# Start addresses of TensorE's operands moved to multiples of 512 bytes, and two small reorderings in the convolution layer of a four-layer decoder

## The chip, the cores and the metric

The kernel runs on one core of one Trainium2 chip. The metric is device time in microseconds (us) of one execution, the median of several runs. A profiled execution of the same program gives the trace; times in it are us from the start of its span, and single instructions are given in ns.

## The reference

Four layers work on x, 256 tokens by 1024 features, fp32. Each layer adds a token mixer and then an MLP with a squared ReLU:

```python
for i in range(DEPTH):                       # DEPTH = 4
    h = _rms_norm(x, attn_norm[i])
    y = mixer[i](h, ...)                     # 0: sparse attention, 1: stick-breaking attention,
                                             # 2: Conformer convolution, 3: block-sparse attention
    x = x + y
    hm = _rms_norm(x, mlp_norm[i])
    x = x + jnp.square(jax.nn.relu(hm @ mlp_w_up[i])) @ mlp_w_down[i]   # 1024 -> 4096 -> 1024
```

The mixer of layer 2, in which code is moved:

```python
a, b = jnp.split(h @ w_in, 2, axis=-1)
u = a * jax.nn.sigmoid(b)                    # gate
u = causal_depthwise_conv(u, dw_w, width=31) + dw_b
un = (u - mean(u)) * rsqrt(var(u) + eps) * ln_g + ln_b
return jax.nn.silu(un) @ w_out
```

## The kernel before

Weights come from HBM in transfers of 1 MB (tile `raw`, 128 partitions by 2048 fp32). ScalarE (ACT) rounds them to fp32r (`wh`, line 157), VectorE (DVE) takes the remainder (`wl`, line 158). Activations are held in the same way as a high and a low part (`xT`, `oT`, `u`). A product of two such numbers is three matmuls: high by high, low by high, high by low. TensorE loads a stationary operand of 128 columns (row kind PEld in the profile) and streams a moving operand of up to 512 columns past it (row kind PE); each matmul here loads its own stationary operand.

The matmuls that matter by name:

- `projT` (line 211, `proj_T`): first half of each MLP and some mixer projections. Stationary: slices of `wh` or `wl`; moving: `xT`, 512 columns with `wh` (high and low part of x in one go) and 256 with `wl`.
- `dn` (lines 190 to 192, `mm3`): second half of each MLP. Stationary: `u`; moving: 512 columns of `wh` or `wl`.
- `proj` (the same lines): mixer projections. Stationary: `xT`; moving: mostly 512 columns of `wh` or `wl`.
- `acc` (lines 218 to 220, `mm3_T`): mixer outputs. `ab` (line 917): the convolution's input product. Both: stationary `wh`/`wl`, moving 256 columns.
- fp32 matmuls (transposes against `ident`, products with `mean`, attention scores) move a column at half the rate, and all of them but the transposes show as two records each.

Tiles are laid out in SBUF one after the other, in the order in which pools and tiles are made: the pool `const` (`xr`, `gains`, `ident`, `nhalf`, `mean`, `identr`), then `rawp`, `hlp` (`wh`, `wl`), `act` (`xT`, `oT`, sums of squares), `sm` (small ones), and above them the pools that one stage opens and closes. So a small tile early on shifts all that follow. All tiles start at multiples of 32 bytes. Read from the built program, in bytes past a multiple of 512:

| tile | before | after |
|---|---|---|
| `wh`, `wl`, `raw` | 416 | 0 |
| `xT`, `oT` | 416 | 0 |
| `u` in the MLPs of layers 0, 2 and 3 | 32 | 0 |
| `u` in the MLP of layer 1 | 96 | 0 |
| `mean`, `identr` | 416 | 0 |
| `ident` | 384 | 0 |
| `qT`, `kT`, `vv`, exponentials of layer 1 | 32 | 0 |
| `un`, `uc` of the convolution | 448 | 352 |

Slices of `wh`, `wl`, `xT` and `u` begin at further multiples of 512 bytes, so they have the tile's remainder. One exception is the fourth chunk of layer 0's projection, 280 columns wide (1120 bytes): there the moving slices for an odd feature tile start at 416 + 1120 = 3 x 512 bytes, and those for an even one at 416.

Each engine executes its own list in order. The lists are made by a scheduling layer from the order of the code and `issue_after`; it may put independent work between.

In `conv`, the norm of the input is needed as a row factor `rbc` before the first gate. `token_stats` makes two tiny products `ms` (sums of squares by `mean`), GpSimd (POOL) raises them to the power -1/2 (`rstd`, line 128), `broadcast_rows` makes `bc` by TensorE. The gate's VectorE, ScalarE and DMA work leads to `us`. After that come `fill` (matmuls whose result nobody reads, line 947), then five steps of 1, 1, 2, 2 and 2 feature tiles: normalise `un` on VectorE (line 953), transpose it on TensorE (line 960), silu on ScalarE (line 963, twice a tile: rounded and exact), the low part on VectorE (line 966). The output product `o.go` reads `oT`; the weights of its second half are split only after the last silu.

Of the kernel before, what the change touches and what calls it, by code (L numbers as in the profile page):

```python
# [10 lines left out]
F32 = mybir.dt.float32  # L11
F32R = mybir.dt.float32r
# [4 lines left out]
P = 128  # L17
# [3 lines left out]
KT = D // P  # L21
# [46 lines left out]
def trunk(ctx: ExitStack, tc: tile.TileContext, A: dict, out: bass.AP):  # L68
    nc = tc.nc
    const = ctx.enter_context(tc.tile_pool(name="const", bufs=1))  # L70
    rawp = ctx.enter_context(tc.tile_pool(name="rawp", bufs=3))
    hlp = ctx.enter_context(tc.tile_pool(name="hlp", bufs=8))
    act = ctx.enter_context(tc.tile_pool(name="act", bufs=2))
    sm = ctx.enter_context(tc.tile_pool(name="sm", bufs=4))
    ps = ctx.enter_context(tc.tile_pool(name="ps", bufs=2, space=bass.MemoryType.PSUM))

    def bank(tag, name):
        return ps.tile([P, 512], F32, tag=tag, bufs=4 if tag == "B" else 2, name=name)


    def start_norm(i):
        n = Norm()
        n.g = gains[:, i]
        n.xT = act.tile([P, KT, 2, NT, P], F32R, tag="aT", name="xT")
        n.s2 = act.tile([P, S], F32, tag="s2", name="s2")
        return n
# [24 lines left out]
    def token_stats(n, tag):  # L111

        o = bank(tag, "ms")
        for t in range(NT):
            nc.tensor.matmul(o[:, 2 * t:2 * t + 2], lhsT=n.s2[:, t * P:(t + 1) * P], rhs=mean[:, 0:2], start=t == 0,
                             stop=t == NT - 1, skip_group_check=True)
        n.me = sm.tile([P, NT], F32, tag="nme", name="nme")
        nc.vector.tensor_scalar(n.me, o[:, 0:2 * NT].rearrange("p (t c) -> p t c", c=2)[:, :, 0], EPS, None,
                                op0=ALU.add)
# [6 lines left out]
    def rstd(n):  # L126
        r = sm.tile([P, NT], F32, tag="rstd", name="rstd")
        nc.gpsimd.tensor_tensor(r, n.me, nhalf[:, :NT], op=ALU.pow)
        return [r[:, t:t + 1] for t in range(NT)]

    def broadcast_rows(dst, cols, tag):

        o = bank(tag, "bc")
        for t in range(NT):
            nc.tensor.matmul(o[:, t * P:(t + 1) * P], lhsT=cols[t].to_broadcast([P, P]), rhs=ident, start=t == 0,
                             stop=t == NT - 1, skip_group_check=True)
        if dst is None:
            return o
        nc.scalar.copy(dst, o[:, :S])
# [75 lines left out]
    def mm3_T(o, w, aT, kt, first, last):  # L215

        wh, wl = w
        nc.tensor.matmul(o, lhsT=wh, rhs=aT[:, kt, 0], start=first, stop=False, skip_group_check=True)  # L218
        nc.tensor.matmul(o, lhsT=wh, rhs=aT[:, kt, 1], start=False, stop=False, skip_group_check=True)  # L219
        nc.tensor.matmul(o, lhsT=wl, rhs=aT[:, kt, 0], start=False, stop=last, skip_group_check=True)  # L220

    class Acc:
# [3 lines left out]
            self.b = {}  # L226

        def add(self, m, w, aT, kt, first, last):
            if m // 2 not in self.b:
                self.b[m // 2] = bank("AC"[m // 4], f"acc{m // 2}")  # L230
            fs = slice(m * P, (m + 1) * P)
            mm3_T(self.tile(m), (w[0][:, fs], w[1][:, fs]), aT, kt, first and m % 2 == 0, last)

        def tile(self, m):
            return self.b[m // 2][:, (m % 2) * S:(m % 2 + 1) * S]

    class Out:
# [13 lines left out]
        def fetch(self, i, eng):  # L251

            self.raws[i] = rawp.tile([P, 2048], F32, tag="raw", name="raw")
            eng.dma_start(self.raws[i], self.src[:, i * 2048:(i + 1) * 2048])

        def go(self, kts, ms):
            last = KT - 1 in kts
# [562 lines left out]
    def conv(n):  # L820
        aT = n.xT
        nxt = start_norm(6)
        with tc.tile_pool(name="cv", bufs=1) as sp, tc.tile_pool(name="cvw", bufs=2) as wp, \
# [11 lines left out]
            rbc = sp.tile([P, S], F32, name="rbc")  # L835
# [69 lines left out]
            for c in range(4):  # L905

                v = ahead.pop(0)
                if c < 3:
                    ahead.append(col_chunk(A["conv_w"], (c + 1) * 4096, 512))
                os_ = [bank("B", "ab") for f in range(2)]  # L910

                def products(f, kts):
                    for i in range(2):
                        fs = slice((2 * i + f) * P, (2 * i + f + 1) * P)
                        for kt in kts:
                            for m, (wi, xi) in enumerate(((0, 0), (0, 1), (1, 0))):
                                nc.tensor.matmul(os_[f][:, i * S:(i + 1) * S], lhsT=v[kt][wi][:, fs],  # L917
                                                 rhs=aT[:, kt, xi], start=kt == 0 and m == 0 and i == 0,
                                                 stop=kt == KT - 1 and m == 2, skip_group_check=True)

                if c == 0:

                    for kts in (range(4), range(4, 8)):
                        for f in range(2):
                            products(f, kts)
                    first = os_
                    continue
                for f in range(2):
                    products(f, range(KT))
                    if c == 1 and f == 0:  # L930
                        token_stats(n, "C")
                        broadcast_rows(rbc, rstd(n), "C")
                        gate(0, first[0])
                        gate(1, first[1])
                    gate(2 * c + f, os_[f])
# [7 lines left out]
            o = outs[0]  # L943

            fill = bank("C", "fill")
            for _ in range(FILL):
                nc.tensor.matmul(fill[:, :P], lhsT=mean, rhs=mean, start=True, stop=True)
            for c0, w in STEPS:
                h = slice(c0, c0 + w)
                un = wp.tile([P, 2, NT, P], F32, tag="ab", name="un")  # L950
                pt = bank("B", "un")
                for e in range(NT):
                    nc.vector.tensor_scalar(un[:, :w, e].rearrange("p k (g q) -> p k g q", q=16),
                                            us[:, h].rearrange("p k (g e q) -> p k e g q", e=2, q=16)[:, :, e],
                                            mv[:, e, 0:1], rs[:, e:e + 1], op0=ALU.subtract, op1=ALU.mult)
                ac = wp.tile([P, 2, S], F32, tag="ac", name="ac")
                for k in range(w):
                    for e in range(NT):
                        x = (NT * k + e) * P
                        nc.tensor.transpose(pt[:, x:x + P], un[:, k, e], ident)  # L960

                    for dst in (oT[:, c0 + k, 0].rearrange("p t c -> p (t c)"), ac[:, k]):
                        a = nc.scalar.activation(dst.rearrange("p (j e) -> p e j", e=2),
                                                 pt[:, k * S:(k + 1) * S].rearrange("p (e j) -> p e j", e=2), AF.Silu,
                                                 scale=cw[:, c0 + k, 2:3], bias=cw[:, c0 + k, 3:4])
                b = nc.vector.tensor_sub(oT[:, h, 1], ac[:, :w].rearrange("p k (t c) -> p k t c", c=P),
                                         oT[:, h, 0].bitcast(F32))
                if c0 + w == LATE:
                    with tc.issue_after(a.ins), tc.issue_after(b.ins):
                        o.load(range(EARLY, 4))  # L970
            raw = rawp.tile([P, 2048], F32, tag="raw", name="raw")
            with tc.issue_after(power.ins):
                nc.gpsimd.dma_start(raw, A["up2"][:, :2048])
            o.go(range(4), range(8))
            o.go(range(4, 8), range(8))
        return nxt, raw

# [1 line left out]
    def moba(n):  # L979
# [114 lines left out]
                o.go(range(4, 8), range(8))  # L1094
        return nxt

    xr = const.tile([P, KT, S], F32, name="xr")
    gains = const.tile([P, 8, KT], F32, name="gains")
    ident = const.tile([P, P], F32, name="ident")
    nc.scalar.dma_start(gains, A["norms"])  # L1100
    nc.scalar.dma_start(ident, A["ident"])
    nhalf = const.tile([P, 4], F32, name="nhalf")
    nc.vector.memset(nhalf, -0.5)
    mean = const.tile([P, P], F32, name="mean")
    nc.vector.memset(mean, 1.0 / D)
    n = start_norm(0)
    feats = list(range(KT))
# [10 lines left out]
    o = bank("C", "warm")  # L1118
    for _ in range(10):
        nc.tensor.matmul(o[:, :P], lhsT=mean, rhs=mean, start=True, stop=True)  # L1120

    identr = const.tile([P, P], F32R, name="identr")
    n = nsa(n, load_x)
    n = mlp(0, n, 1)
    n = stick(n)
    taps = {}
    with tc.tile_pool(name="taps", bufs=1) as tapp:
        tp = tapp.tile([P, KT, 64], F32, name="tp")
        nc.sync.dma_start(tp, A["conv_taps"])
        eye = tapp.tile([P, 16], F32, name="eye")  # L1130
        nc.sync.dma_start(eye, A["eye16"])
        n = mlp(1, n, 2, lambda j: taps_tile(j) if j < 4 else None)
        n, raw = conv(n)
    n = mlp(2, n, 3, None, raw)
    n = moba(n)
# [121 lines left out]
```

## Time and profile before

| | |
|---|---|
| median of 3 runs | 1180.42 us (1180.06 to 1180.87) |
| the profiled execution | 1180.44 us |
| its span, first to last instruction of the program | 1178.7 us |
| TensorE busy | 1167.1 us, 7046 records |
| VectorE, ScalarE busy | 782.9 us, 620.9 us |
| HBM read | 207.74 MB |

A matmul's record lasts from its start to the modelled end of its result, and the next one starts while it lasts; records overlap. The busy share of TensorE therefore says that it is hardly ever empty, not how fast it streams. What one matmul costs the ones behind it is the time from its start to the next start, called its step below. It is read from the start times of a first and a last row and the count between them.

### The profile page before, as it was taken

How to read it: one execution, taken by the hardware profiler on the slowest of the kernel's cores; microseconds unless marked ns; L12 is line 12 of the kernel's file. 1: busy time of each engine (PE TensorE's matmuls, PEld its weight loads, DVE VectorE, ACT ScalarE, POOL GpSimd, SP SyncE). 2: the span in 40 equal slices, each digit the busy share in tenths (PEclk: the TensorE clock that was granted, in tenths of full speed). 3: DMA queues.
4: the chain of work that ended last, by engine and by line, in shares of the span. 5: the costliest groups of instructions: out<-in, count | busy, mean ns of one | idle time of the engine just before them, and what ended most of it. 6: DMA issues, size and time to landing. Idle time of an engine off the chain costs nothing.

```text
span 1178.7 us, 17661 instructions
## 1 busy us (share of the span) xinstructions
PE 1167.1 (99%) x7046; PEld 1008.7 (86%) x7046; DVE 782.9 (66%) x1206; ACT 620.9 (53%) x1031; POOL 33.2 (3%) x50
## 2 busy tenths in 40 slices
PE   9999999999999999999999999999999999999998
PEld 6798988888888998888889998888888889888886
DVE  7788675656585686656665677656659886656553
ACT  6487554444565654544563275454446665544441
POOL 1100000000000000000001100000001100000000
PEclk9999999999999999999999999999999999999999
DMA  8554255545454436545545746455455543555440
GB/s 303 203 186 144 77 210 214 185 172 204 154 201 163 144 129 222 190 183 198 188 151 165 251 172 222 164 197 212 153 195 178 182 162 118 187 214 192 165 178 36
DMA packets 35650, 211.11 MB, mean 179 GB/s; under 512 B 4592, under 2 KB 7664, under 8 KB 12016
## 3 DMA queue, kind: packets, MB, share of 16 engines
q1 hardware_dynamic: 31104, 198.76, 47.0%
q0 software_dynamic: 1568, 6.80, 2.1%
q10 hardware_dynamic: 2896, 4.42, 1.1%
q8 instruction: 55, 0.90, 0.3%
q14 instruction: 27, 0.22, 0.1%
HBM read 207.74 MB, written 2.23 MB: 178 GB/s over the span
## 4 chain that ended last, share of the span: by engine, by line
PE 67%; issue 26%; DVE 3%; ACT 2%; DMA 1%; POOL 1%; SPq 0%; POOLq 0%; ACTq 0%; DVEq 0%
PE projT L211 23%; PE dn L190 8%; PE dn L192 8%; PE dn L191 8%; PE ab L917 2%; PE proj L192 2%; PE proj L191 2%; PE proj L190 2%; PE acc L218 2%; PE acc L220 2%; PE acc L219 2%; DVE wl L158 1%; PE po L675 1%; ACT wh L157 1%; PE cv L859 1%
## 5 line engine op out<-in xcount | busy, mean ns | idle before, releaser
L158 DVE TENSOR_TENSOR wl<-raw,wh 128x1024 fp32r<-128x1024 f32 (+1 forms) x372 | 441.1, 1212 | 186.9 <-ACT wh L157 182.8
L157 ACT CAST wh<-raw 128x1024 fp32r<-128x1024 f32 (+1 forms) x372 | 376.1, 1041 | 215.6 <-PE dn L192 111.2
L211 PE MATMUL projT<-xT,wh 128*128 128x512 f32 x1152 | 361.5, 396 | 0.3 <-DVE xT L101 0.3
L211 PEld LDWEIGHTS projT<-xT,wl 128*128 128x128 f32 x1152 | 215.3, 188 | 49.9
L211 PE MATMUL projT<-xT,wl 128*128 128x256 f32 x1152 | 225.4, 278 | 0.0
L190 PE MATMUL dn<-wh,u 128*128 128x512 f32 x512 | 202.7, 396 | 0.0
L192 PE MATMUL dn<-wh,u 128*128 128x512 f32 x512 | 202.0, 395 | 0.0
L191 PE MATMUL dn<-wl,u 128*128 128x512 f32 x512 | 201.4, 393 | 0.0
L211 PEld LDWEIGHTS projT<-xT,wh 128*128 128x128 f32 x1152 | 178.2, 189 | 3.7 <-DVE xT L101 0.5
L192 PEld LDWEIGHTS dn<-wh,u 128*128 128x128 f32 x512 | 96.4, 188 | 22.4
L191 PEld LDWEIGHTS dn<-wl,u 128*128 128x128 f32 x512 | 96.4, 188 | 20.7
L190 PEld LDWEIGHTS dn<-wh,u 128*128 128x128 f32 x512 | 96.5, 188 | 20.4
L316 ACT COPY b<-projT 128x256 f32<-128x256 f32 x128 | 41.2, 374 | 93.7 <-PE projT L211 93.4
L191 PE MATMUL proj<-wl,xT 128*128 128x512 f32 (+2 forms) x224 | 85.9, 384 | 2.5 <-DVE wl L158 2.1
L190 PE MATMUL proj<-wh,xT 128*128 128x512 f32 (+2 forms) x224 | 85.7, 385 | 0.4 <-ACT wh L165 0.3
L317 DVE TENSOR_TENSOR s<-projT,b 128x256 f32<-128x256 f32 x128 | 48.2, 418 | 55.0 <-ACT b L316 55.0
L192 PE MATMUL proj<-wh,xT 128*128 128x512 f32 (+2 forms) x224 | 84.5, 378 | 0.0
L89 ACT CAST u<-q 128x1024 fp32r<-128x1024 f32 x32 | 33.6, 1049 | 82.9 <-DVE q L319 82.7
L218 PE MATMUL acc<-oT,wh 128*128 128x256 f32 x256 | 73.8, 292 | 0.0
L219 PE MATMUL acc<-oT,wh 128*128 128x256 f32 x256 | 72.7, 285 | 0.0
L220 PE MATMUL acc<-oT,wl 128*128 128x256 f32 x256 | 71.2, 284 | 0.0
L90 DVE TENSOR_TENSOR u<-q,u 128x1024 fp32r<-128x1024 f32 x32 | 39.2, 1226 | 34.5 <-ACT u L89 34.5
(231 smaller groups left out, 1252.6 us busy)
## 6 DMA issues: line engine op xcount, KB each, us to landing
raw<-in_down SPq DMA_DIRECT2D x64, 1024.0 KB, 4.8
raw<-in_up SPq DMA_DIRECT2D x63, 1024.0 KB, 4.8
raw<-in_sb_w SPq DMA_DIRECT2D x12, 1024.0 KB, 4.8
raw<-in_moba_w SPq DMA_DIRECT2D x12, 1024.0 KB, 4.9
raw<-in_conv_w SPq DMA_DIRECT2D x8, 1024.0 KB, 4.7
st<-dr POOLq DMA_DIRECT2D x16, 287.0 KB, 6.3
raw<-in_nsa_w SPq DMA_DIRECT2D x4, 1024.0 KB, 5.9
rawc<-in_nsa_cmp SPq DMA_DIRECT2D x4, 1024.0 KB, 4.8
```

The costliest lines, as they stand in the source:

```text
L90: return a, nc.vector.tensor_sub(lo, src, hi.bitcast(F32))
L157: nc.scalar.copy(wh[:, :w], r)
L158: nc.vector.tensor_sub(wl[:, :w], r, wh[:, :w].bitcast(F32))
L190: nc.tensor.matmul(o, lhsT=aT[:, kt, 0, t, :], rhs=wh, start=first, stop=False)
L191: nc.tensor.matmul(o, lhsT=aT[:, kt, 0, t, :], rhs=wl, start=False, stop=False)
L192: nc.tensor.matmul(o, lhsT=aT[:, kt, 1, t, :], rhs=wh, start=False, stop=last)
L211: nc.tensor.matmul(o[:, :width], lhsT=v[kt][part][:, f * P:(f + 1) * P], rhs=rhs, start=kt == 0 and part == 0, stop=kt == KT - 1 and part ...
L218: nc.tensor.matmul(o, lhsT=wh, rhs=aT[:, kt, 0], start=first, stop=False, skip_group_check=True)
L219: nc.tensor.matmul(o, lhsT=wh, rhs=aT[:, kt, 1], start=False, stop=False, skip_group_check=True)
L220: nc.tensor.matmul(o, lhsT=wl, rhs=aT[:, kt, 0], start=False, stop=last, skip_group_check=True)
L316: nc.scalar.copy(b, o[:, S:])
L317: nc.vector.tensor_add(s[:, f], o[:, :S], b)
```

## The change

Tiles are reordered, widened or added so that the operands of the large matmuls start at multiples of 512 bytes (table above). An unused tile `front` of 384 bytes stands ahead of `const`, one named `back` of 384 bytes follows `sm`; `ident`, `identr` and `mean` stand next to each other, `nhalf` is widened to 256 bytes and `eye` to 512. Of the program's 6523 matmuls none had both operands at a multiple of 512 before, and 5866 have after.

In `conv`, `token_stats` and `rstd` move ahead of the products of the second chunk. `Out.begin` issues the 24 output matmuls of the first feature tile in the middle of the five steps, and the transposes of the third step may only be issued behind the first 16 of them.

```diff
+    edge = ctx.enter_context(tc.tile_pool(name="edge", bufs=1))
+    edge.tile([P, 96], F32, name="back")
...
+        def begin(self, parts):
+            for wi, xi in parts:
+                for m in range(KT):
+                    p = nc.tensor.matmul(self.acc.tile(m), lhsT=self.w[0][wi][:, m * P:(m + 1) * P],
+                                         rhs=self.aT[:, 0, xi], start=wi + xi == 0 and m % 2 == 0, stop=False,
+                                         skip_group_check=True)
+            return p
...
+                if c == 1:
+                    token_stats(n, "C")
+                    rows = rstd(n)
                 for f in range(2):
                     products(f, range(KT))
                     if c == 1 and f == 0:
-                        token_stats(n, "C")
-                        broadcast_rows(rbc, rstd(n), "C")
+                        broadcast_rows(rbc, rows, "C")
...
-                        nc.tensor.transpose(pt[:, x:x + P], un[:, k, e], ident)
+                        with ExitStack() as behind:
+                            if c0 == 2:
+                                behind.enter_context(tc.issue_after(begun[0].ins))
+                            nc.tensor.transpose(pt[:, x:x + P], un[:, k, e], ident)
...
+                if c0 < 2:
+                    begun.append(o.begin(((0, 0), (1, 0)) if c0 == 0 else ((0, 1),)))
...
-            o.go(range(4), range(8))
+            o.go(range(1, 4), range(8))
...
+    const.tile([P, 96], F32, name="front")
     xr = const.tile([P, KT, S], F32, name="xr")
+    ident = const.tile([P, P], F32, name="ident")
+    identr = const.tile([P, P], F32R, name="identr")
+    mean = const.tile([P, P], F32, name="mean")
     gains = const.tile([P, 8, KT], F32, name="gains")
-    nhalf = const.tile([P, 4], F32, name="nhalf")
+    nhalf = const.tile([P, 64], F32, name="nhalf")
...
-        eye = tapp.tile([P, 16], F32, name="eye")
+        eye = tapp.tile([P, P], F32, name="eye")[:, :16]
```

On TensorE's list of the program before, at the end of the first half of the second chunk of `conv`, the sums `ms` and the broadcast `bc` stand close together among the products `ab`:

```order
L917 MATMUL ab<-xT,wl 128x256
L115 MATMUL ms<-mean,s_4340 128x2 x2
L917 MATMUL ab<-xT,wh 128x256 x2
L917 MATMUL ab<-xT,wl 128x256
L917 MATMUL ab<-xT,wh 128x256
L135 MATMUL bc<-ident,rstd 128x128 x2
L917 MATMUL ab<-xT,wh 128x256
```

Of the changed program, TensorE's list near the start of that chunk's products (three rows) and near the end of their first half (three rows):

```order
L928 MATMUL ab<-xT,wl 128x256
L117 MATMUL ms<-mean,s_4345 128x2 x2
L928 MATMUL ab<-xT,wh 128x256 x2
...
L928 MATMUL ab<-xT,wl 128x256
L137 MATMUL bc<-ident,rstd 128x128 x2
L928 MATMUL ab<-xT,wh 128x256 x2
```

The two `ms` products moved up by 42 products `ab`, and `bc` by 4.

On TensorE's list of the program before, at the convolution's output behind `fill` (`un` is the transposes of the five steps, `acc` the output's matmuls, the number that of an accumulator):

```order
L947 MATMUL fill<-mean 128x128 x11
L960 MATMUL un<-ident,un 128x128 x8
L218 MATMUL acc_6847<-oT,wh 128x256
L218 MATMUL acc_6854<-oT,wh 128x256
L218 MATMUL acc_6861<-oT,wh 128x256
L218 MATMUL acc_6868<-oT,wh 128x256
```

The same place of the changed program:

```order
L960 MATMUL fill<-mean 128x128 x11
L977 MATMUL un<-ident,un 128x128 x4
L262 MATMUL acc_6782<-oT,wh 128x256 x2
L262 MATMUL acc_6785<-oT,wh 128x256 x2
...
L262 MATMUL acc_6791<-oT,wh 128x256 x2
L977 MATMUL un<-ident,un 128x128 x4
L220 MATMUL acc_6782<-oT,wh 128x256
```

The third step's four transposes stood with the first four; now 24 output matmuls (12 rows of 2, of which nine are left out) stand between.

## Rows read from the trace of the kernel before

**Rows 1.** The page's head and busy times (us, share of span, records).

```profile
span 1178.7 us, 17661 instructions
PE 1167.1 (99%) x7046; PEld 1008.7 (86%) x7046; DVE 782.9 (66%) x1206; ACT 620.9 (53%) x1031; POOL 33.2 (3%) x50
```

**Rows 2.** Busy time in one MLP block of layer 2, with granted clock.

```profile
750.38:772.68 22.30, 22.30 (x114) 18.77 (x113) 13.41 (x15) 10.34 (x14) 0.00 (x0) 1.00 0.52 189
```

**Rows 3.** Groups by line and shape: count, busy us, mean ns of a record, idle.

```profile
L211 PE MATMUL projT<-xT,wh 128*128 128x512 f32 x1152 | 361.5, 396 | 0.3 <-DVE xT L101 0.3
L211 PE MATMUL projT<-xT,wl 128*128 128x256 f32 x1152 | 225.4, 278 | 0.0
L190 PE MATMUL dn<-wh,u 128*128 128x512 f32 x512 | 202.7, 396 | 0.0
L218 PE MATMUL acc<-oT,wh 128*128 128x256 f32 x256 | 73.8, 292 | 0.0
...
L190 PE MATMUL proj<-wh,xT 128*128 128x512 f32 x176 | 69.6, 398 | 0.4 <-ACT wh L165 0.3
```

**Rows 4.** Timeline of TensorE, MLP of layer 2: start, length, line, operands.

```profile
741.79 0.39 PE L211 MATMUL projT<-xT,wl 128*128 128x256 f32 x2
...
750.38 0.39 PE L190 MATMUL dn<-wh,u 128*128 128x512 f32 x1
...
761.54 0.39 PE L211 MATMUL projT<-xT,wh 128*128 128x512 f32 x1
```

**Rows 5.** Timeline of TensorE, MLP of layer 1: first `dn`, and the row behind the 48th.

```profile
497.66 0.40 PE L190 MATMUL dn<-wh,u 128*128 128x512 f32 x1
...
508.66 0.39 PE L211 MATMUL projT<-xT,wh 128*128 128x512 f32 x1
```

**Rows 6.** Timeline of TensorE, 48 `proj` matmuls of layer 3 (the first, three others).

```profile
906.02 0.48 PE L190 MATMUL proj<-wh,xT 128*128 128x512 f32 x1
...
907.73 0.39 PE L191 MATMUL proj<-wl,xT 128*128 128x512 f32 x1
...
909.31 0.39 PE L192 MATMUL proj<-wh,xT 128*128 128x512 f32 x1
...
916.79 0.39 PE L192 MATMUL proj<-wh,xT 128*128 128x512 f32 x1
```

**Rows 7.** Longest pieces of the chain that ended last: start, length, what.

```profile
198.26 11.14 PE projT L211 x64
...
629.79 16.78 PE ab L917 x140
```

**Rows 8.** Timeline of TensorE: fp32 matmuls, 128 columns at half rate.

```profile
676.44 2.62 PE L947 MATMUL fill<-mean 128*128 128x128 f32 x22
...
935.43 1.36 PE L1062 MATMUL pp<-ident,p 128*128 128x128 f32 x11
```

**Rows 9.** Timeline of TensorE, 280-column chunk: six matmuls even tile, six odd.

```profile
45.09 0.29 PE L190 MATMUL proj<-wh,xT 128*128 128x280 f32 x1
...
45.86 0.29 PE L190 MATMUL proj<-wh,xT 128*128 128x280 f32 x1
...
46.63 0.29 PE L190 MATMUL proj<-wh,xT 128*128 128x280 f32 x1
```

**Rows 10.** Timeline around the broadcast of the norm in the convolution layer.

```profile
621.80 0.41 DVE L109 TENSOR_TENSOR s<-s,sq 128x256 f32<-128x256 f32 x1
...
628.35 0.28 PE L917 MATMUL ab<-xT,wh 128*128 128x256 f32 x1
629.08 0.71 PE L135 MATMUL bc<-ident,rstd 128*128 128x128 f32 x4 [0.45 <-POOL rstd L128]
```

**Rows 11.** Timeline at the start of the convolution's output, behind `fill`.

```profile
678.94 2.46 PE L960 MATMUL un<-ident,un 128*128 128x128 f32 x8
679.57 0.58 ACT L963 ACTIVATE oT<-un,cw 128x256 fp32r<-128x256 f32 x1 [0.78 <-PE un L960]
...
681.16 0.61 PE L218 MATMUL acc<-oT,wh 128*128 128x256 f32 x3
```

More of the change, by code (lines that the diff above doesn't have):

```diff
@@ L228, in add @@
         def add(self, m, w, aT, kt, first, last):
-            if m // 2 not in self.b:
-                self.b[m // 2] = bank("AC"[m // 4], f"acc{m // 2}")
             fs = slice(m * P, (m + 1) * P)
@@ L234, in tile @@
         def tile(self, m):
+            if m // 2 not in self.b:
+                self.b[m // 2] = bank("AC"[m // 4], f"acc{m // 2}")
             return self.b[m // 2][:, (m % 2) * S:(m % 2 + 1) * S]
@@ L947, in conv @@
                 nc.tensor.matmul(fill[:, :P], lhsT=mean, rhs=mean, start=True, stop=True)
+            begun = []
             for c0, w in STEPS:
@@ L1095, in moba @@
         return nxt
+    const.tile([P, 96], F32, name="front")
     xr = const.tile([P, KT, S], F32, name="xr")
+    ident = const.tile([P, P], F32, name="ident")
+    identr = const.tile([P, P], F32R, name="identr")
+    mean = const.tile([P, P], F32, name="mean")
     gains = const.tile([P, 8, KT], F32, name="gains")
-    ident = const.tile([P, P], F32, name="ident")
     nc.scalar.dma_start(gains, A["norms"])
     nc.scalar.dma_start(ident, A["ident"])
-    nhalf = const.tile([P, 4], F32, name="nhalf")
+    nhalf = const.tile([P, 64], F32, name="nhalf")
     nc.vector.memset(nhalf, -0.5)
-    mean = const.tile([P, P], F32, name="mean")
     nc.vector.memset(mean, 1.0 / D)
@@ L1120, in trunk @@
         nc.tensor.matmul(o[:, :P], lhsT=mean, rhs=mean, start=True, stop=True)
-    identr = const.tile([P, P], F32R, name="identr")
     n = nsa(n, load_x)
```

## The prediction

> **What bounds the kernel now.** I read the head first: TensorE is busy for 1167.1 of 1178.7 us [rows 1], so at most 11.6 us of the span are free of it, and whatever shortens the kernel must shorten TensorE's own steps or the few waits between them. Then the windows by stage: in a 22.30 us block of an MLP TensorE is busy throughout, VectorE for 13.41 and ScalarE for 10.34 us, the DMA engines for 0.52 of the time, at granted clock 1.00, the upper level of 2.4 GHz [rows 2]. Here nothing stands close behind TensorE: it could shrink by a third before VectorE became the limit. Eight such blocks make an MLP, four MLPs most of the kernel.
>
> Then the steps. Between 750.38 and 761.54 stand 48 `dn` matmuls: 11.16 / 48 = 232.5 ns each [rows 4]. 512 columns at one column a cycle of 2.4 GHz are 213.3 ns (an estimate from the granted clock). The fp32 matmuls give the overhead on top: 11 transposes of 128 columns, two cycles a column, last 1.36 us, less one record of 0.27 that is 10 steps of 109 ns, 2 ns over 106.7 [rows 8]. So a 512-column matmul without friction would take some 215.5 ns, one of 256 columns 109. Every large group lies above that:
>
> - `dn`, layers 0, 2, 3 (1152 matmuls, u at 32): 232.5 [rows 3, 4]
> - `dn`, layer 1 (384, u at 96): 497.66 to 508.66, 11.00 / 48 = 229.2 [rows 5]
> - `proj`, 512 columns (3 x 176 = 528, `xT` at 416): 906.02 to 916.79, 10.77 / 47 = 229.1; the seven steps from 907.73 to 909.31 take 1.58 / 7 = 225.7 [rows 3, 6]
> - `projT` (2304, half of 512 and half of 256 columns): 11.14 / 64 = 174.1 against 162 [rows 3, 7]
> - `acc` and `ab`, 256 columns (3 x 256 and 384): 16.78 / 140 = 119.9 [rows 3, 7]
>
> The sum of these excesses is 1152 x 17.0 + 384 x 13.7 + 528 x 13.6 + 2304 x 12.1 + 1152 x 10.9 ns = 19.6 + 5.3 + 7.2 + 27.9 + 12.6 = 72.6 us. That is the most that the addresses can give.
>
> **Do addresses bear on the step?** One comparison says yes. `dn` is the same code in all four MLPs, with the same moving operand; in layer 1 `u` starts at 96 past a multiple of 512, elsewhere at 32, and the step is 229.2 instead of 232.5 [rows 4, 5]. VectorE, ScalarE and DMA do the same work in both. So 64 bytes of the stationary operand's start are worth 3.3 ns or 1.4%. One comparison says that not every address counts: in the 280-column chunk six matmuls whose moving operand starts at 416 take 45.86 - 45.09 = 0.77 us, and the next six, whose moving operand starts at 0, take 46.63 - 45.86 = 0.77 [rows 9]. The moving operand's start alone gives nothing there (1120 bytes from either start cross two multiples of 512). A stationary operand at 0 is nowhere in this trace.
>
> By the Trainium skill ("TensorE: Matmul & The Clock Gate", Part 2, step 1) TensorE has two independent SBUF read ports, so that loading the next weights takes no bandwidth from the running matmul. The step's dependence on the stationary operand's start [rows 4, 5] does not fit that. The same page ("Wait — 56ns, not 53.3ns?") measures 215.7 ns for 512 columns, with no condition on addresses; by it the large matmuls would have 72 us to lose, and it does not say to what.
>
> **The change, part by part.** *Alignment.* 5866 of 6523 matmuls now have both operands at 0. The trace bounds the new step from below by the friction-free one and from above by today's, or by the slow value of the rival below. I take the shortest regular stretches seen: 226 ns for 512 columns [rows 6]; 113 for 256 behind 256 in `projT`, from two records that last 0.39 together, less one of 0.278 [rows 3, 4]; so (226 + 113) / 2 = 169.5 for `projT`. For `acc` and `ab` every window is short, and the next load of 128 stationary columns must fit into it; such loads back to back, beside a half-rate stream, take (2.62 - 0.275) / 21 = 111.7 ns [rows 8] (0.275 is one record's length). Between 119.9 and 111.7 I take 116. The gains: 1152 x 6.5 = 7.5; 384 x 3.2 = 1.2; 528 x 3.1 = 1.6; 2304 x 4.6 = 10.6; 1152 x 3.9 = 4.5; together 25.4 us. The 96 matmuls of 384 columns and the small ones add under 1 us and are left out.
>
> The waits do not come to light when TensorE gets 2% faster: in a block VectorE has 8.9 us of slack [rows 2]. Unused tiles cost no instruction; a wider `nhalf` is one memset at the start, beside the first transfers.
>
> *The norm's sums ahead of the second chunk.* Today `bc` waits for POOL's `rstd`: the product before it starts at 628.35 and `bc` at 629.08, 0.73 us where a step of 0.12 would do [rows 7, 10]. 0.6 us go. Moved up by 42 products of 119.9 ns, 5.0 us, `ms` comes to stand at some 622.5; its last input is added from 621.80 to 622.21 [rows 10]. A faster TensorE in front of it (100 products at 4 ns less) brings it to 622.1, a wait of 0.1. The bounds: -0.6 to +0.5. Nothing stands behind it on TensorE that others wait for sooner. I take -0.6.
>
> *The first output tile ahead of the third step's transposes.* Today eight transposes last from 678.94 to 681.16, paced by VectorE's normalising; at 109 ns they would need 0.87 of the 2.22 us [rows 8, 11]. In the new order four run in front, then the first `acc` waits for ScalarE's first silu (679.57 + 0.58 = 680.15), so TensorE starts at some 680.2; 16 `acc` are over at 682.1 and 8 more at 683.1, and the four transposes then run unpaced in 0.44. To have done eight transposes and 24 `acc`: before 681.16 + 24 x 0.12 = 684.0, after 683.1 + 0.5 = 683.6. Gain 0.4. In return the third step's silu waits until 683.2 instead of starting at 681.4 (ScalarE's next but two instruction), and so does all behind it on ScalarE: the later silus and the split of the second half's weights. That has cover as long as 72 `acc` of the first half are left (8.6 us); if the cover is short at its end, up to 1 us comes back. Bounds -0.4 to +1.0, I take -0.4.
>
> Sum, against the profiled execution of 1180.44 us, which lies 0.02 from the median: 1180.4 - 25.4 - 0.6 - 0.4 = 1154 us.
>
> **The rivals.** *Only the distance counts.* The step may depend on the distance between the stationary and the moving operand's start modulo 512, not on either: 128 gives 232.5, 192 gives 229.2, and `proj` at 0 gives 229.1 [rows 4 to 6]. For it: these three, and the 280-column chunk where the moving start alone did nothing. Against it: `projT` has distance 0 as well and is no better. Then only `dn` of three layers gains, 1152 x 3.4 = 3.9 us, and with the 1.0 of the convolution the time is 1175.5.
>
> *Nothing.* 416 mod 32 is 0 like all others, and the excess may come from the full-rate stream of fp32r itself, with the difference between 32 and 96 an accident of where VectorE's and ScalarE's tiles lie beside `u`. For it: 280 columns [rows 9]. Then 1179.4. By the Trainium skill ("SBUF — State Buffer", the note on SBUF cachelines) only crossings of 16-byte lines matter, and all starts before and after are multiples of 32, so this rule gives the same result; the 3.3 ns between `u` at 96 and at 32 do not agree with it.
>
> *Slower: 0 is like 32.* 128 columns from 32 reach the next multiple of 512 after 480 bytes, from 96 after 416, from 416 after 96 bytes, and the steps fall in that order: 232.5, 229.2, 229.1 [rows 4 to 6]. A start at 0 reaches it after 512 and continues the row on the bad side. At least 528 x 3.4 + 384 x 3.3 = 3.1 us then come on top, 1182.5 with the convolution's gain; if `projT`, `acc` and `ab`, today at 416, also slow by the same 1.5% (2.6 ns and 1.8 ns), 2304 x 2.6 + 1152 x 1.8 = 8.1 us more: 1190.6. It decides if a `dn` step is above 232.5.
>
> **How the numbers follow.** Chances: alignment shortens the steps to about the shortest ones seen or further 0.52; distance only 0.18; nothing 0.14; slower 0.16. 0.2% of this kernel, 2.4 us, is about what a measurement can tell from no change. Faster by more than that: the first two, 0.70. Same: the third, and no part of the rest, 0.14. Slower: 0.16. The first case's own range is 1120 to 1170 (half of 25.4 us gone, or most of the 72.6 there). The range over all that leaves out no more than 2 in 10 is 1120 to 1182: it holds the first three cases but for the deep end of the first, and leaves out the slower one.
>
> **What would show it.** In the changed kernel's timeline, 48 `dn` should last 10.85 us, 64 `projT` matmuls 10.85, and 140 `ab` products 16.2; layers 0 and 1 should show the same `dn` step. 229 in `dn` with 174 in `projT` means distance only; 232.5 and 229.2 as before, nothing; over 232.5 in both, the slower rival. `bc` should have no wait for POOL; `acc` should start near 680.2 less what was won before. I am wrong on the convolution if TensorE waits for `wl` in the second half of `acc`. The prediction is wrong as a whole if a stationary operand at 0 costs what one at 416 does.

## The result

The changed kernel takes 1171.93 us (median of 6 runs), the kernel before 1180.24 (6 runs): a ratio of 0.993, 95% interval 0.9915 to 0.9944. It is 8.3 us faster, where 26.4 were forecast. One of the six runs of each is far slower (1633.35 us at a granted clock of 0.655, and 1425.09); the ratio and the interval are of the others. The measured time lies in the stated range but is a third of the forecast gain.

### The profile page after: what moved, and what is told of

The parts are those of the page before. It is cut to its first block, busy times and chain, and to the rows that moved or that the text cites. A ratio compares the mean times of both kernels' runs of the same rounds, so it can differ in the third digit from the quotient of the medians.

```text
span 1170.3 us, 17657 instructions
## 1 busy us (share of the span) xinstructions
PE 1159.3 (99%) x7046; PEld 1007.8 (86%) x7046; DVE 782.7 (67%) x1206; ACT 621.6 (53%) x1031; POOL 33.7 (3%) x50
## 4 chain that ended last, share of the span: by engine, by line
PE 94%; DVE 2%; ACT 2%; DMA 1%; POOL 0%; issue 0%; SPq 0%; ACTq 0%; DVEq 0%; POOLq 0%
PE projT L213 34%; PE dn L192 10%; PE dn L194 10%; PE dn L193 10%; PE ab L928 4%; PE proj L194 3%; PE proj L193 3%; PE proj L192 3%; PE acc L220 3%; PE acc L222 3%; PE acc L221 3%; PE po L686 1%; PE cv L870 1%; DVE wl L160 1%; DMA raw<-in_nsa_w 1%; PE sc L648 1%
## 5 line engine op out<-in xcount | busy, mean ns | idle before, releaser
L192 PE MATMUL dn<-wh,u 128*128 128x512 f32 x512 | 200.3, 391 | 0.0
L194 PE MATMUL dn<-wh,u 128*128 128x512 f32 x512 | 199.5, 390 | 0.0
L220 PE MATMUL acc<-oT,wh 128*128 128x256 f32 x248 | 71.8, 291 | 0.0
L221 PE MATMUL acc<-oT,wh 128*128 128x256 f32 x248 | 70.5, 285 | 0.0
```

What stands on the lines that cost most here:

```text
L192: nc.tensor.matmul(o, lhsT=aT[:, kt, 0, t, :], rhs=wh, start=first, stop=False)
L194: nc.tensor.matmul(o, lhsT=aT[:, kt, 1, t, :], rhs=wh, start=False, stop=last)
```

## The profile after

The head of the changed kernel's page, as [rows 1]; then groups by line and shape, as [rows 3] (count, busy us, mean ns of a record, idle):

```profile
span 1170.3 us, 17657 instructions
PE 1159.3 (99%) x7046; PEld 1007.8 (86%) x7046; DVE 782.7 (67%) x1206; ACT 621.6 (53%) x1031; POOL 33.7 (3%) x50
```

```profile
L213 PE MATMUL projT<-xT,wh 128*128 128x512 f32 x1152 | 361.6, 396 | 0.3 <-DVE xT L103 0.3
L213 PE MATMUL projT<-xT,wl 128*128 128x256 f32 x1152 | 225.5, 278 | 0.0
L192 PE MATMUL dn<-wh,u 128*128 128x512 f32 x512 | 200.3, 391 | 0.0
```

The span is 8.4 us shorter, TensorE's busy time 7.8; the other engines do what they did. Of the large groups one record has become shorter, that of `dn` (396 to 391 ns); `projT` stands where it stood (396 and 278).

The timeline of TensorE in layer 1 (first `dn` and the row behind the 48th, as [rows 5]) and the chain's pieces of `projT` and `ab`, as [rows 7]:

```profile
495.38 0.40 PE L192 MATMUL dn<-wh,u 128*128 128x512 f32 x1
...
506.27 0.39 PE L213 MATMUL projT<-xT,wh 128*128 128x512 f32 x1
```

```profile
197.74 11.14 PE projT L213 x64
...
625.66 17.27 PE ab L928 x144
```

48 `dn` last 10.89 us, 226.9 ns each from start to start, and the mean of all steps is 227.1, in layer 1 as in layers 0 and 2 (226.9 in layer 3; 11.16 and 11.00 before, [rows 4, 5]). 64 `projT` last 11.14 as before, and `ab` takes 17.27 / 144 = 119.9 ns as before. 10.85, 10.85 and 16.2 for 140 (115.7 each) were promised: the first came about, the other two did not move at all.

Starts of the same matmuls in both traces, subtracted, give the account by stage. The changed kernel is ahead by 0.04 us when MLP 0 begins, and wins 2.04 us in MLP 0, 0.86 in MLP 1, 1.17 in the convolution, 2.06 in MLP 2 and 2.14 in MLP 3; in the stick-breaking layer (layer 1) and the block-sparse attention (layer 3) it wins 0.1 together. 2.04 us are 384 `dn` matmuls times 5.3 ns (232.4 to 227.1), 2.14 are 383 times 5.5 (232.4 to 226.9) and a rest, 0.86 are 384 times 2.0 (229.1 to 227.1) and a rest.

In the convolution the matmuls of `ab` behind `bc` are 0.71 us further ahead than those in front of `ms`; 0.34 us of the 1.17 come from a wait of the gated part near 670 us that differs from run to run (0.1 and 0.17 in the two pairs of runs below). The timeline there, as [rows 10]:

```profile
619.57 0.51 PE L117 MATMUL ms<-mean,s 128*128 128x2 f32 x4
621.93 0.70 POOL L130 TENSOR_TENSOR rstd<-nme,nhalf 128x2 f32<-128x2 f32 x1 [287.11 <-DVE nme L120]
...
625.05 0.60 PE L137 MATMUL bc<-ident,rstd 128*128 128x128 f32 x4
```

`rstd` is ready at 622.63, 2.4 us before `bc` starts, and `bc` waits for nothing. At the output, as [rows 8, 11]:

```profile
672.46 2.62 PE L960 MATMUL fill<-mean 128*128 128x128 f32 x22
...
674.96 1.10 PE L977 MATMUL un<-ident,un 128*128 128x128 f32 x4
...
676.21 1.21 PE L262 MATMUL acc<-oT,wh 128*128 128x256 f32 x8 [0.16 <-ACT oT L980]
...
679.18 0.60 PE L977 MATMUL un<-ident,un 128*128 128x128 f32 x4
679.60 0.59 ACT L980 ACTIVATE oT<-un,cw 128x256 fp32r<-128x256 f32 x1 [2.05 <-PE un L977]
```

`acc` starts 1.25 us behind the first transpose, as worked out (678.94 to 680.2). From `fill` to the first `dn` of MLP 2 it is 51.45 us (672.46 to 723.91) against 51.57 (676.44 to 728.01): the move gives 0.12 us. It repeats: of the traces here six with the whole move have 51.43 to 51.46 us there, five without it 51.56 to 51.68.

## The experiments

Theory **D** is the first rival of the prediction, widened: the step depends on the distance between the starts of the stationary and the moving operand, not on multiples of 512. Theory **Z**: the stationary operand's own start decides. All starts are modulo 512. The runs without a ratio are single executions; they are read by their steps. Their spans also hold differences from waits in layer 0, where the same code differs from run to run: the first `dn` starts between 163.15 and 164.83 us in the traces below.

**Addresses alone, convolution alone.** The first run takes the two moves of the convolution out of the changed kernel; the second puts only them into the kernel before.

> The changed kernel with the convolution put back as it was: the addresses alone. If what the profiles show stage by stage is right (2.0, 0.85, 2.05 and 2.0 us won in the dn steps of the four MLPs), it is 6.9 us faster than before, 1173.5 us, and the changed kernel lies 1.2 us below it. If the addresses and the moved convolution steps act on each other, the sum of this gain and of the next run's is not 8.3 us.

> The kernel before with the two moves in the convolution alone, every address as before. By the stage table 0.7 us from the norm's sums and 0.45 from the output tile: 1179.2 us. A dn step of 232.4 ns in layers 0, 2 and 3 and 229.1 in layer 1, as before.

1172.87 us, ratio 0.9941 (0.9929 to 0.9954), and 1178.97 us, ratio 0.9991 (0.9982 to 1.0). The gains are 7.0 and 0.9 us, together 7.9 of 8.3. Both parts do what the stages show, and do not act on each other beyond what the measurement can tell; the interval of the second reaches 1.0, so its 0.9 us rest on the stages rather than on the times.

**`u` moved alone, in the kernel before.** An unused tile ahead of `u`, in bytes by layer:

```diff
+                if (384, 416, 64, 448)[i] and j == 0:
+                    mp.tile([P, (384, 416, 64, 448)[i] // 4], F32, tag="pad", bufs=1, name="pad")
                 u = mp.tile([P, 4, 2, NT, P], F32R, tag="u", name="u")
```

> The kernel before with u alone moved, to 416, 0, 96 and 480 past a multiple of 512 in MLP 0, 1, 2 and 3; wh and wl stay at 416, so the distance u minus wh is 0, 96, 192 and 64. Theory D (only the distance modulo 512 counts): MLP 0 has the step of the changed kernel, 227.1 ns (48 dn in 10.89 us), MLP 2 229.1, and MLP 1 is above 227.1. Theory Z (the start of the stationary operand itself counts, 32 is bad, 96 half as bad, 0 is good): MLP 1 has 227.1 and MLP 2 229.1; MLP 0 is open. MLP 1 tells them apart. If the layer rather than the address made the difference, MLP 1 stays at 229.1 and MLP 2 at 232.4.

The timeline in MLP 0 (`u` at 416) and MLP 1 (`u` at 0), first `dn` and the row behind the 48th:

```profile
186.44 0.40 PE L190 MATMUL dn<-wh,u 128*128 128x512 f32 x1
...
197.33 0.39 PE L211 MATMUL projT<-xT,wh 128*128 128x512 f32 x1
...
473.44 0.39 PE L190 MATMUL dn<-wh,u 128*128 128x512 f32 x1
...
484.68 0.39 PE L211 MATMUL projT<-xT,wh 128*128 128x512 f32 x1
```

MLP 1 is the worst of all, 11.24 us for 48, a mean of 234.2 ns, with a stationary operand at a multiple of 512. MLP 0, with both operands at 416, has the changed kernel's 227.1 (48 from 186.44 to 197.33, 10.89). MLP 2 has 229.1 with `u` at 96 and distance 192, like layer 1 of before. Z falls, D stands. The total, 1179.05 us (0.9995, 0.9986 to 1.0004), adds up two better and two worse layers.

**`u` moved alone, in the changed kernel.** The same tile with 32, 64, 96, 128, then 160, 192, 224, 256, then 320, 384, 448, 480 bytes in MLP 0 to 3.

> The changed kernel with u alone moved, to 32, 64, 96 and 128 past a multiple of 512 in MLP 0, 1, 2 and 3; wh and wl stay at 0, so these are the distances too. Theory D: MLP 3 (distance 128) has 232.4 ns as layers 0, 2, 3 of before, MLP 1 (64) and MLP 2 (96) repeat the steps of MLP 3 and MLP 1 of the run with u moved in the kernel before. Theory Z: MLP 0 (u at 32) has 232.4 and MLP 2 (u at 96) 229.1.

> The changed kernel with u at 160, 192, 224 and 256 past a multiple of 512 in MLP 0 to 3, wh and wl at 0. Theory D: MLP 1 (distance 192) has the 229.1 ns of layer 1 of before; 160 lies between 232.4 and 229.1 if the step is a smooth curve of the distance. Theory Z has no reason for 229.1 in MLP 1.

> The changed kernel with u at 320, 384, 448 and 480 past a multiple of 512 in MLP 0 to 3, wh and wl at 0: the rest of the curve. If the step depends on how the loads of 128 stationary columns (512 bytes) and the moving stream meet modulo 512, the curve is not flat here; if the distance matters only up to 192, all four are at 227.1 ns.

1181.5 us (1.0013, 1.0004 to 1.0022), 1177.64 and 1179.9. Mean `dn` steps by distance, of these runs, the one before and the two kernels:

| `u` minus `wh` | step, ns | seen at (`u`, `wh`) |
|---|---|---|
| 0, 256 | 227.1, 226.9 | (0, 0), (416, 416); (256, 0) |
| 32 | 233.2 | (32, 0) |
| 64, 320 | 233.3, 233.4 | (64, 0), (480, 416); (320, 0) |
| 96 | 234.2 | (96, 0), (0, 416) |
| 128, 384 | 232.5 | (128, 0), (32, 416); (384, 0) |
| 160 | 233.3 | (160, 0) |
| 192, 448 | 229.1 | (192, 0), (96, 416); (448, 0) |
| 224, 480 | 233.3 | (224, 0); (480, 0) |

The last rows of MLP 3 in the run with 256, the first and the 48th `dn`:

```profile
1061.91 0.40 PE L192 MATMUL dn<-wh,u 128*128 128x512 f32 x1
...
1072.57 0.39 PE L194 MATMUL dn<-wh,u 128*128 128x512 f32 x1
```

(1072.57 - 1061.91) / 47 = 226.8 ns. So the distance counts modulo 256, not 512; the same distance from other starts gives the same step within 0.2 ns. The curve is not smooth: 192 is good, 160 and 224 on both sides of it are not.

By the Trainium skill ("SBUF — State Buffer", the note on SBUF cachelines) each crossing to a new 16-byte line pays a penalty. That makes starts that are multiples of 32 alike; all these are, and the steps differ by 7 ns: the trace does not agree.

**`u` to 416 and nothing else.** The kernel before, with an unused tile of 384, 320, 384 and 384 bytes ahead of `u` in MLP 0 to 3.

> The kernel before with nothing but u moved, to 416 past a multiple of 512 in all four MLPs, where wh and wl start; no operand of a product is at a multiple of 512, and the convolution is as before. If the step hangs on the distance alone and the rest of the realignment is worth nothing: 227.1 ns in all four MLPs and 6.9 us less than before, the time of the run with the addresses alone. If multiples of 512 give something elsewhere, less than that.

1172.96 us, ratio 0.9939 (0.9925 to 0.9952), and 227.1 ns in the four MLPs (226.9 in the last; 48 `dn` from 186.40 to 197.29, 10.89 us, as in the changed kernel): the whole gain of the addresses (1172.87 above), with no matmul that has both operands at a multiple of 512. The other matmuls that the change brought to such starts (some 4300 of 5866) gave nothing that can be measured; in their large groups the operands had equal starts before.

**`xT` and `oT` moved alone, in the changed kernel.** A tile of so many bytes ahead of `act`, and `back` shortened by as much, so that `u` and `wh` stay at 0. The other tiles of `act` and the small ones of `sm` move along:

```diff
+    gap = ctx.enter_context(tc.tile_pool(name="gap", bufs=1))
+    gap.tile([P, 32], F32, name="gap")
     act = ctx.enter_context(tc.tile_pool(name="act", bufs=2))
...
-    edge.tile([P, 96], F32, name="back")
+    edge.tile([P, 64], F32, name="back")
```

> The changed kernel with xT and oT alone moved, to 128 past a multiple of 512, against wh and wl at 0: the distance that cost dn 5.3 ns, now in proj (xT stationary), projT and ab (xT moving) and acc (oT moving). Theory D for every fp32r matmul: proj goes from 227 to 232.4 ns (528 of them, 2.9 us), and projT, ab and acc become slower by some ns as well, with 12 ns for a pair of projT (that would be 13.8 us in all). If dn's step is something of its own, nothing moves. If the direction counts (stationary behind moving), proj moves and projT, ab and acc do not.

> The changed kernel with xT and oT at 96 past a multiple of 512, the distance that was worst for dn (234.2 ns). If what counts is which operand is the stationary one, proj (activations stationary) rises from 227 to 234, and projT, ab and acc (weights stationary) stay at 349 ns for a pair of 512 and 256, and at 120. If they only happen to be blind to 128, a pair of projT rises by some ns, 1152 x that.

> The changed kernel with xT and oT at 32: a point of the curve for weights as the stationary operand. A pair of projT has 348.9 ns at distance 0, 349.3 at 128, 353.6 at 96. If 0 is the lowest point for projT too, the pair lies between 349 and 354 here; if below 348, a kernel that is faster than both is in reach.

> The same with xT and oT at 64: a pair of projT between 349 and 354 ns if 0 is its lowest point; proj (activations stationary) at 233 as dn at 64.

> The changed kernel with xT and oT at 160. If the curve of ab and acc goes evenly from 119.3 at 128 to 115.6 at 192, 117.5 here; if neighbouring points say nothing of each other, as 64 (116.8) and 96 (119.9) do, anything between 115 and 121. dn at 160 had 233.3, so proj is at 233.

> The same with xT and oT at 192, the third best distance of dn (229.1): proj at 229; a pair of projT at some 350 if its curve has the shape of dn's.

1173.34 us (0.9946, 0.9932 to 0.996) at 128; single executions 1179.29 at 96, 1170.82 at 32, 1168.38 at 64, 1176.01 at 160 and 1167.14 at 192. Mean steps in ns, without those more than a quarter longer than their columns need; a pair is the mean step of 512 and of 256 columns together:

| `xT` minus `wh` | `proj` 512 | `projT` pair | `ab` | `acc` | span, us |
|---|---|---|---|---|---|
| 0 (changed kernel) | 227.8 | 348.3 | 119.9 | 119.6 | 1170.3 |
| 32 | 233.2 | 347.1 | 117.0 | 117.1 | 1169.0 |
| 64 | 233.3 | 345.9 | 116.8 | 117.6 | 1166.6 |
| 96 | 234.1 | 353.0 | 119.9 | 119.8 | 1177.5 |
| 128 | 232.5 | 348.8 | 119.3 | 118.6 | 1171.3 |
| 160 | 233.3 | 351.7 | 118.4 | 118.4 | 1174.2 |
| 192 | 229.7 | 347.1 | 115.6 | 115.8 | 1165.3 |

`proj` with 512 columns follows the curve of `dn`. `dn` itself, whose operands do not move here, has 227.1 to 227.7 ns, so up to 0.6 ns of a mean does not come from its own two operands. The 128 run alone looked as if only `proj` and `dn` depended on the distance (the third reading in its expectation); the 96 run takes that back, a pair of `projT` rises by 4.7 ns. Where the weights are stationary the curve is another one, and 0 is not its best point: 0 is among the worst for `ab` and `acc`. Not every form follows either curve: in the 280-column chunk of [rows 9], where an even feature tile has distance 0 and an odd one 160 (modulo 256), the mean steps are 129.8 and 130.0 ns before, and 127.0 to 129.0 in all these runs, where 512 columns differ by 6. The chain's pieces at 96:

```profile
175.12 11.30 PE projT L215 x64
```

and at 192:

```profile
174.84 11.11 PE projT L215 x64
...
623.25 16.33 PE ab L930 x144
```

**The version that beats both, timed.** The kernel with `xT` and `oT` at 192 once more, in 4 runs.

> The kernel with u at wh's start and xT, oT at 192, timed in rounds. By the steps of its one look against the changed kernel (ab and acc 115.7 instead of 119.8 ns, 1152 of them: 4.7 us; a pair of projT 347.1 instead of 348.3, 1152 pairs: 1.4; proj 229.7 instead of 227.8, 528: minus 1.0) it is 5.1 us faster than the changed kernel: 1166.8, a ratio of 0.989 to before.

1167.68 us, ratio 0.99 to before (0.9883 to 0.9916): 11.8 us less than before, where the changed kernel has 8.3 less; between the two kernels that is 3.5 us by these gains and 4.2 by the times (1171.93), and 5.1 were expected. `ab` 115.8, `acc` 114.9, a pair of `projT` 347.1. The piece of 144 `ab` lasts 16.96 us in this trace and 16.33 in the single execution before: at this distance the step of a stretch is not the same in each execution, while at 0 the 144 take 17.27 in each trace that has them in one piece.

```profile
622.50 16.96 PE ab L930 x144
```

**What lies above 215.5 ns.** First the second and third `dn` of each three cut to fewer stationary columns (the first four lines of the diff); then, in another run, all three alike, and in MLP 0 a constant bf16 tile (behind the mark):

```diff
-        nc.tensor.matmul(o, lhsT=aT[:, kt, 0, t, :], rhs=wl, start=False, stop=False)
-        nc.tensor.matmul(o, lhsT=aT[:, kt, 1, t, :], rhs=wh, start=False, stop=last)
+        nc.tensor.matmul(o[:c], lhsT=aT[:, kt, 0, t, :c], rhs=wl, start=False, stop=False)
+        nc.tensor.matmul(o[:c], lhsT=aT[:, kt, 1, t, :c], rhs=wh, start=False, stop=last)
...
+        if bf:
+            for i, (x, y) in enumerate(((0, wh), (0, wl), (1, wh))):
+                nc.tensor.matmul(o, lhsT=ones[0][:, :P], rhs=ones[0][:, P:],
+                                 start=first and i == 0, stop=last and i == 2)
```

> The changed kernel with the second and third dn matmul of each three cut to the first 96, 64, 32 and 8 stationary columns in MLP 0 to 3 (so the output is not the reference's); the moving operand keeps 512 columns. Of the 227.1 ns step 11.6 lie above the 215.5 of a matmul without friction. If the weight load that runs beside a step costs it these 11.6 ns in proportion to its columns, the first step of three (beside it the load of the cut one) falls to 224, 221, 218 and 216 ns, and the third (beside it a full load) stays at 227. If it is a fixed price per matmul or of the fp32r stream, all stay at 227.1.

> The changed kernel with dn altered (so the output is not the reference's): in MLP 0 all dn matmuls take a constant bf16 tile, 128 stationary and 512 moving columns; in MLP 1, 2 and 3 nine of every twelve dn matmuls (three of four feature blocks) are cut to 96, 64 and 32 stationary columns, all three of a triple alike. What lies above 215.5 ns in a dn step at its best (227.1) is open after the first eight runs. Theory L (the price of a weight load beside the stream, by its bytes): MLP 0 has half the bytes and comes to some 221; the cut ones to 224, 221 and 218. Theory F (the fp32r form itself has a fixed price): MLP 0 has 215.5, and the cut ones stay at 227. Theory P (the step is set by how load and stream meet, as the distance is): the cut ones move up or down without order, like the 232.1, 229.5, 230.1 and 233.3 of the mixed triples, and MLP 0 is near 215.5.

Mixed triples of 96, 64, 32 and 8 columns have mean steps of 232.1, 229.5, 230.1 and 233.3 ns; in the other run, between cut matmuls alone, 96, 64 and 32 columns have 229.8, 229.4 and 231.8. No mean is below the 227.1 of the full load, so the excess is not a price that falls with the load's size, and it is not constant either. The bf16 `dn` in the timeline:

```profile
185.44 10.31 PE L196 MATMUL dn<-ones 128*128 128x512 bf16 x47
```

46 steps and a record of 0.39: (10.31 - 0.39) / 46 = 215.7 ns, each of them 215 or 216. With 128 stationary and 512 moving columns and a load at every matmul, bf16 has no excess; fp32r has at least 11.3 ns. But that run changes more than the form of the stream: every matmul reads the same constant tile, at one distance (256 bytes), with half the bytes a column, and its weight loads last half as long:

```profile
L196 PEld LDWEIGHTS <-ones 128*128 128x128 bf16 x384 | 37.1, 98 | 43.5
...
L203 PEld LDWEIGHTS dn<-wh,u 128*128 128x128 f32 x108 | 20.4, 188 | 7.6
```

The loads' length alone is not it, since an fp32r load of 32 columns lasts 109 ns in the same trace and has 231.8 ns steps. Which of the rest takes the excess away is not shown. By the Trainium skill ("TensorE: Matmul & The Clock Gate", "Wait — 56ns, not 53.3ns?") 512 columns take 215.7 ns: the bf16 steps agree, and no fp32r step of these runs does. The shortest fp32r step with 512 columns in any of these traces is 224 ns.

**The output move.** The changed kernel without it, and with 16 instead of 24 matmuls ahead of the third step (the diff is of the second):

```diff
-                if c0 < 2:
-                    begun.append(o.begin(((0, 0), (1, 0)) if c0 == 0 else ((0, 1),)))
+                if c0 == 0:
+                    begun.append(o.begin(((0, 0), (1, 0))))
...
+            o.begin(((0, 1),))
             o.go(range(1, 4), range(8))
```

> The changed kernel with the convolution's output put back as it was, the norm's sums still moved: by the stage table the stretch from the first transpose of the output to the next MLP is 0.12 us longer than in the changed kernel, with 0.9 of it lost up to the last acc of the first tile and 0.8 regained after that. If the output move had won my 0.4, 0.4.

> The changed kernel with 16 acc matmuls instead of 24 ahead of the third step's transposes; the other 8 follow the last step. The third step's first silu starts 1 us earlier (679.6 less 1.0 on the changed kernel's scale). If its lateness is what gives the gain back in the second half, the stretch is shorter than the changed kernel's by up to 0.3 us; if the weights' split or the stores of the features are what the second half waits for whatever ScalarE does, it is as long or longer, since 8 matmuls of cover are gone at the start.

From `fill` to the first `dn` of MLP 2 these take 51.57 us (671.88 to 723.45) and 51.41 (671.25 to 722.66), the changed kernel 51.45. So the move is worth 0.12 us. With the third step's first silu 0.94 us earlier (3.70 instead of 4.64 us behind the first transpose) the stretch changes by 0.04, about the spread of the traces with the move. That its lateness takes the rest back is not borne out; as this run also moves eight matmuls behind the last step, it is not excluded. The 0.9 and 0.8 of the expectation were misread: the pairing behind them set transposes of different steps against each other. Counted from the first transpose, 37 `acc` and 14 transposes are done after 7.09 us in the changed kernel and after 7.52 before, which is the 0.43 that was won.

## Why the prediction was right and wrong

**The step that failed** is the choice of the new steps under *Alignment*: "the shortest regular stretches seen" for every group whose operands come to 0, "so (226 + 113) / 2 = 169.5 for `projT`", 116 for `acc` and `ab`, 226 for `proj`. 16.7 of the 25.4 us hang on these groups, whose two operands had the same remainder before (416) and have it after (0). Their steps did not move: a pair of `projT` has 348.5 ns before and 348.3 after, `ab` 119.9 in both, `acc` 119.7 and 119.6, `proj` 228.1 and 227.8. What the runs show in its place is that the distance between the two starts counts, and not multiples of 512: `u` moved alone to the remainder of `wh`, 416, has the whole gain of the addresses. The 113 of `projT` is the short one of a pattern whose long ones pay for it: four steps in a row are 233, 236, 116 and 112 ns in the changed kernel. And the sum of 72.6 us, "the most that the addresses can give", counts as the addresses' what no start tried here takes away: at its best distance `dn` keeps 11.6 of its 17.0 ns and `ab` 6.6 of its 10.9. What that remainder is stays open; bf16 `dn` has none of it, with the reservations above. Term by term:

- `dn`: 8.7 forecast, 1152 x 5.3 + 384 x 2.0 = 6.9 measured. The step came to 227.1 instead of 226.
- `proj`: 1.6 forecast, nothing measured. Its two operands stood at equal starts already; the 229.1 of [rows 6] holds some longer steps among those of 226.
- `projT` 10.6 and `acc`, `ab` 4.5 forecast, nothing measured: distance 0 before and after. The 116 ns assumed for `acc` and `ab` do exist (115.6), but at a distance of 192, which the change does not set.

**The rival that was right** is "only the distance counts", held at 0.18. Its one argument against itself, that `projT` "has distance 0 as well and is no better", took the excess that stays at every distance for a sign of a bad address. One of its arguments for itself speaks against it: in the 280-column chunk the moving start alone changes the distance too (0 and 160 modulo 256), and the steps there are 0.2 ns apart, where `dn` shows 6; the rival does not hold for every form. Its size was off too: 1175.5 came from counting layer 1's distance of 192 as good as 0 (2.0 ns missed in 384 steps), and from `proj`'s 229.1 as the step at distance 0, where it is 227.1 (3.4 ns instead of 5.3 in 1152). With these two and the convolution's measured 0.83 it gives 1180.4 - 6.9 - 0.8 = 1172.7. The rest of the measured 8.3 is as small as the differences between executions.

**The other rivals.** "Nothing" falls with the 5.3 ns. "0 is like 32" falls: `u` at 0 has 227.1 or 234.2 ns by where `wh` stands. The comparison of 32 and 96 [rows 4, 5] was read rightly as one of addresses; it was a comparison of the distances 128 and 192, which the text named but put behind.

**The convolution.** The norm's sums: 0.6 forecast, 0.71 measured, and `bc` without a wait as promised. The output: 0.4 forecast, 0.12 measured. The start of `acc` and the late silu came as worked out, and after 37 `acc` 0.43 us had been won. 0.31 of it was given back later, some 0.17 of that between 690.4 and 691.6, where three steps of `acc` are 0.06 to 0.10 us too long and there is one of 0.10 before; the run with the convolution's moves alone has the same three. No wait for `wl` or anything else is on record there. What causes it is open.

## What to carry to other kernels

Before an address is rounded, measure the step at several distances between the two operands of the largest matmul group: here one unused tile of 384 bytes (320 in layer 1) ahead of `u` gave all that the realignment gave. Equal starts modulo 256 were best where activations were stationary, and not where weights were; each group wants its own sweep. An excess over a friction-free step is no gain in reach until some row or run shows the same form without it.

## What was not expected of the hardware

- The start-to-start time of an fp32r matmul with 512 columns depends on the distance between its operands' starts modulo 256 bytes: 226.9 to 234.2 ns, with no smooth curve (192: 229.1; 160 and 224: 233.3). `proj` with 512 columns has the same curve; with 280 columns no dependence shows (127.0 to 130.0 ns).
- With the roles of weights and activations exchanged the curve is another one: `ab` and `acc` have 119.9 ns at 0 and 96 and 115.6 at 192; a pair of `projT` 345.9 at 64 and 353.0 at 96.
- bf16 with the same 128 and 512 columns, on one constant tile, has 215.7 ns, fp32r 226.9 at best on average, and loading fewer stationary columns (96 to 8) made the fp32r step longer, 229.4 to 233.3 ns.

No run tried what mechanism makes the distance count.
